# Three tiles side by side, chunk by chunk, at the start of each half of a projection

## The chip, the cores and the metric

The kernel runs on one core of a Trainium2 chip. The metric is the time of one execution on the device in microseconds (us); lower is better. Times of the kernel before are the median of three runs. One further execution was recorded by the hardware profiler, and all rows below come from it.

## The reference

A trunk of two decoder layers is run for one prompt (512 positions) and for 8 samples of 8 positions each (64 rows), 576 columns in all, with a width of 1024. The reference in its bare shape:

```python
h = rmsnorm(x, norm_mix_pre)
m = mixer(h)                         # even layer: attention and S5; odd layer: Mamba-2
x = x + rmsnorm(m, norm_mix_post)
h = rmsnorm(x, norm_mlp_pre)
a = relu(h @ w_up)                   # 1024 -> 4096
x = x + rmsnorm((a * a) @ w_down, norm_mlp_post)
```

Layer 0 is even, layer 1 is odd; each is followed by the MLP of the last three lines. All arithmetic is f32. `rmsnorm` divides every column by the root of its mean square, so nothing that reads `h` of a column can start before the sum of squares over all 1024 features of `x` is there.

## The kernel before

**Products.** Activations lie transposed: features on the partitions in 8 chunks of 128, positions along the free axis, cut into two halves of 288 columns (`HV`). Each f32 product is made of three matmuls in a rounded f32 form, `wh*xh`, `wh*xl` and `wl*xh`, where `h` is the rounded value and `l` the rest (L326, L347, L348). One output tile of 128 features by 288 columns is 3 x 8 chunks = 24 matmuls into one PSUM bank. The pool `mm`, from which `project3_steps` takes its banks, has three banks in this part of the program (`LATE_BANKS`, L1592); a fourth tile can start only when the bank of the first has been read.

**Weights.** For each tile SP's queue loads a 128 x 1024 block (`w`); ACT rounds it to `wh` (L290), VectorE (DVE) subtracts to `wl` (L312). A pair `wh`, `wl` serves both halves.

**Half by half.** `rounds(..., first=n)` makes one round in which `n` tiles are run for half 0 and then the same `n` tiles for half 1. There are three such stretches: the first segment of each MLP's up product (`LEAD` = 8 tiles) and the start of the odd layer's input projection (`lead`, five tiles: 40, 32, 36, 16, 17). Elsewhere a tile's two halves follow one another. A half-by-half stretch stands where the columns of half 1 are not ready yet: while half 0 is multiplied, the post-norm and pre-norm of half 1 run on the other engines. These are, in `add_normed` and what it calls, eight scalings `m = m * normw * nr` on DVE (L381), eight additions to the residual (L395; chunks 1, 4 and 7 on POOL, the others on DVE), eight weightings `h` on ACT and DVE (L403), squares on ACT with sums on POOL and DVE (L203), and two small matmuls `rstd` (L211) that add the squares over the partitions.

**Evacuation.** In `up` DVE reads the bank first (`m` or `a2t` = max(ps, 0) times the column's factor, L1006), ACT squares (L287), ACT and DVE split into two parts (L290, L355), and in half 1 POOL takes differences (L1014). POOL also forms sums and differences of the down weights (`ws`, L1070). After the eighth tile of half 1 `down_pairs` begins. In the odd layer the lead's first tile (40) is the raw time step `dtr` (L1172), from which a chain on DVE leads to `dt_post` (L1247).

**Order.** Every engine works through its own list in order. The lists are fixed when the program is built: a scheduler simulates the program and orders the instructions of each engine, so a change in one place can move instructions on all of them.

Of the kernel before, what the change touches and what calls it, by code (L numbers as in the profile page):

```python
# [21 lines left out]
HV = ((0, HALF), (HALF, T))  # L22
# [195 lines left out]
class _Kernel:  # L218
# [106 lines left out]
                    es.enter_context(self.tc.issue_after(ins))  # L325
            self.nc.tensor.matmul(*args, **kw)  # L326

    def project3(self, *args):
        for _ in self.project3_steps(*args):
            pass  # L330

    def project3_steps(self, src, rounds, kchunk, evac, ready=None, ring=lambda m: None):


        for steps in rounds:
            parts, ready = ready or {}, None
            for m, hf in steps:
                if m not in parts:
                    parts[m] = self.split_block(src(m), ring(m))
                wh, wl = parts[m]  # L340
                lo, hi = HV[hf]
                ps = self.mmps("project3")
                out = ps[:, : hi - lo]
                for c in range(8):
                    xh, xl = kchunk(c, hf)
                    self.product(c, out, wh[:, c, :], xh, start=(c == 0), stop=False)
                    self.nc.tensor.matmul(out, wh[:, c, :], xl, start=False, stop=False)  # L347
                    self.nc.tensor.matmul(out, wl[:, c, :], xh, start=False, stop=(c == 7))  # L348
                self.groups += 1
                evac(m, hf, out)  # L350
                yield

    def split_into(self, hi, lo, t):
        self.copy_a(hi, t)
# [70 lines left out]
    def even(self):  # L425
# [3 lines left out]
        with ExitStack() as es:  # L429
# [5 lines left out]
            for _ in range(N_WARM):  # L435
                nc.tensor.matmul(ps[:, :128], self.ones, self.ones, start=True, stop=True)
            self.wp = ev, NSE
            w = a["w_in_e"]
# [155 lines left out]
    def attn_sample(self, pair, qk, qbd, pnew):  # L594
# [8 lines left out]
        def ring():  # L603
            nb[0] += 1
            ways = RINGS[pair]
            return {"k": (self.eb, "kv", NKV), "w": None, "h": (ev, "wh", NSE), "l": (ev, "wl", NSE)}[ways[nb[0] % len(ways)]]

# [377 lines left out]
    def mlp(self, layer, h, r, mx, done):  # L985

        m = self.halves(self.mring)
        nc = self.nc  # L990
        sums = [_Squares(self, 8, SQ_M[hf]) for hf in range(2)]
        up_w, dn_w = self.a[f"w_up{layer}"], self.a[f"w_dn{layer}"]
        e1 = [mx.tile([128, HALF], F32, tag=f"e1{i}", name=self.nm("e1"), bufs=1) for i in range(4)]
        for seg in range(4):
            last = seg == 3
            act = {k: [mx.tile([128, 4 * HALF], F32R, tag=f"a{k}{p}", name=self.nm(f"a{k}"), bufs=1)
                       .rearrange("p (a b) -> p a b", a=4) for p in "hl"]
                   for k in (("11", "21", "22", "t1") if last else ("11", "21", "22", "t1", "t2", "t3", "t4"))}
            names = {(0, 0): "11", (1, 0): "21", (0, 1): "t1", (1, 1): "22"}
            keep = {}  # L1000

            def up(i, hf, ps):
                kh, j = divmod(i % 8, 4)

                t = m[0][:, i, :] if seg == 0 and hf == 0 else mx.tile([128, HALF], F32, tag="a2t", name=self.nm("a2t"), bufs=NC)
                nc.vector.scalar_tensor_tensor(t, ps, 0.0, r[hf], op0=ALU.max, op1=ALU.mult)  # L1006
                self.act(t, t, ACTF.Square)
                keep[kh, hf, j] = t
                part = lambda k: [p[:, j, :] for p in act[k]]
                if last or (kh, hf) != (0, 1):  # L1010
                    self.split_into(*part(names[kh, hf]), t)
                if not last and hf == 1:

                    sub = lambda o, a, b: nc.gpsimd.tensor_tensor(o, a, b, ALU.subtract)  # L1014
                    if kh == 0:
                        t1 = keep["t1", j] = mx.tile([128, HALF], F32, tag="a2t", name=self.nm("a2t"), bufs=NC)
                        sub(t1, t, keep[0, 0, j])
                        self.split_into(*part("t1"), t1)
                    else:
                        t1, b12, b21 = keep["t1", j], keep[0, 1, j], keep[1, 0, j]  # L1020
                        sub(t1, t, t1)
                        self.split_into(*part("t2"), t1)
                        sub(b12, t, b12)
                        self.split_into(*part("t3"), b12)
                        sub(b21, b21, t1)
                        self.split_into(*part("t4"), b21)

            mts = [8 * seg + i for i in ((0, 4, 1, 5, 2, 6, 3, 7) if not last else range(8))]
            self.share = 0 if seg else SHARE_LEAD
            if seg == 0:  # L1030
                self.spare = [2, 3, 4]
            self.project3(lambda i: up_w[i, 0], self.rounds(mts, first=0 if seg else LEAD), self.chunk(h), up)

            if not last:
                self.down_pairs(lambda i: dn_w[i, seg], act, m, e1, seg == 0, mx)
                continue
            self.spare = [2, 3, 4]

            for i in range(4):
                for o in (m[0][:, 2 * i + 1, :], m[1][:, 2 * i, :], m[1][:, 2 * i + 1, :]):  # L1040
                    nc.gpsimd.tensor_tensor(o, o, e1[i], ALU.add)

            def down(i, hf, ps):
                out = m[hf][:, i, :]
                nc.vector.tensor_tensor(out, out, ps, ALU.add)
                sums[hf].add(out)
                if i == 7:
                    done(hf, m[hf], sums[hf])

            self.project3(lambda i: dn_w[i, seg], self.rounds(range(8), last=TAIL),  # L1050
                          lambda c, hf: [p[:, c % 4, :] for p in act[names[c // 4, hf]]], down)
# [60 lines left out]
    def odd(self, h, spill, done):  # L1112
# [3 lines left out]
        with ExitStack() as es:  # L1116
            ol = es.enter_context(tc.tile_pool(name="ol", bufs=1, reuse_waits="tile"))
            od = es.enter_context(tc.tile_pool(name="od", bufs=1, reuse_waits="tile"))
            self.od = od
            self.wp = es.enter_context(tc.tile_pool(name="ow", bufs=1, side="right", reuse_waits="tile")), NSO  # L1120
            self.share = SHARE_ODD
# [73 lines left out]
            hc = self.chunk(h)  # L1195
            src = lambda m: a["w_dt"][0, 0] if m == 40 else w[m, 0]
# [74 lines left out]
            m = self.halves(self.mring)  # L1271
# [31 lines left out]
            lead = [40, 32, 36, 16, 17]  # L1303
            ready = {m: self.split_block(src(m)) for m in lead[:NSO]}
            ow = self.wp
            with tc.tile_pool(name="ld", bufs=1, reuse_waits="tile") as ld:
                self.wp, self.share = (ld, len(lead) - NSO), SHARE_LEAD
                self.project3(src, self.rounds(lead, first=len(lead)), hc, evac, ready)
            self.oa = es.enter_context(tc.tile_pool(name="oa", bufs=1, reuse_waits="tile"))
            self.wp, self.share = ow, SHARE_ODD  # L1310
            proj([18, 19])
# [297 lines left out]
SQ_G = "pv"  # L1609
NS = 5  # L1610
NSE = 2
NSO = 2
NHB = 4
SHARE_ODD = 3
# [31 lines left out]
LEAD = 8  # L1646
# [40 lines left out]
```

## Time and profile before

| | us |
|---|---|
| Median of 3 runs | 1770.38 |
| Lowest, highest | 1768.38, 1774.1 |
| Profiled execution, its own time | 1776.06 |
| Its span | 1773.9 |
| PE busy (TensorE matmuls) | 1665.1 (94%) |
| DVE busy (VectorE) | 1190.5 (67%) |
| ACT busy (ScalarE) | 770.9 (43%) |
| POOL busy (GpSimd) | 670.4 (38%) |

Shares of busy time are means over stages that differ. A stretch is read from its own rows: on PE a bracket at the end of a row gives the idle time just ahead of it and the instruction that ended it. The span begins at 0; the stretches that the change touches lie at about 386 to 436 us (first MLP), 790 to 850 us (odd layer) and 1355 to 1418 us (second MLP).

### The profile page before, as it was taken

Reading aid. Unit: us, or ns where it says so; the run is one execution under the profiler, and the core shown is the slowest. Engines: PE = TensorE matmul, PEld = TensorE weight load, DVE = VectorE, ACT = ScalarE, POOL = GpSimd, SP = SyncE. Lnnn points to the kernel's source line nnn. Section 1 sums busy time; section 2 is a strip of 40 time slices with the busy share of each in tenths; the row PEclk is TensorE's granted clock in tenths of the full one; section 3 lists DMA queues with packets and bytes.
Section 4 is the critical chain, followed back from the end, with each engine's and each line's share of the span. In section 5 each row is a group of like instructions: output and inputs, shape, how many; then the busy total and the mean of one; then the engine's idle time right before and its main releaser. Section 6 shows DMA issues by size and latency. Waiting matters only on the chain.

```text
span 1773.9 us, 31866 instructions
## 1 busy us (share of the span) xinstructions
PE 1665.1 (94%) x12719; PEld 1532.1 (86%) x12719; DVE 1190.5 (67%) x2045; ACT 770.9 (43%) x1506; POOL 670.4 (38%) x705
## 2 busy tenths in 40 slices
PE   8998999899999999998799899999977999999997
PEld 8875565799999999997789789899857999999996
DVE  8656434467668676358788866977667866767634
ACT  5233433455554444334325536335245555344431
POOL 3533100245445362034365434442344644436102
PEclk9999899899999999999899999999978999999999
DMA  8568554530232313223142141241513033231311
GB/s 276 108 227 308 187 191 163 183 97 13 84 107 72 120 48 120 84 67 111 48 139 82 48 161 60 81 147 53 188 59 126 29 93 98 72 119 48 120 59 54
DMA packets 81652, 197.42 MB, mean 111 GB/s; under 512 B 20352, under 2 KB 32000, under 8 KB 81504
## 3 DMA queue, kind: packets, MB, share of 16 engines
q1 hardware_dynamic: 57568, 174.72, 29.8%
q10 hardware_dynamic: 23936, 20.67, 4.0%
q8 instruction: 100, 1.64, 0.4%
q14 instruction: 48, 0.39, 0.1%
HBM read 176.92 MB, written 18.44 MB: 110 GB/s over the span
## 4 chain that ended last, share of the span: by engine, by line
PE 38%; DVE 7%; ACT 2%; POOL 2%; issue 1%; DMA 1%; DVEq 0%; ACTq 0%; POOLq 0%
PE project L326 7%; PE project L347 7%; PE project L348 7%; PE pair L1100 2%; PE pair L1101 2%; PE pair L1102 2%; PE out_proj L1291 2%; PE out_proj L1289 2%; PE out_proj L1290 2%; PE ssd_group L1499 1%; DVE m L381 1%; DVE wl L312 1%; PE ssd_group L1420 1%; PE ssd_group L1454 1%; DVE cacc L1143 1%
## 5 line engine op out<-in xcount | busy, mean ns | idle before, releaser
L326 PE MATMUL project<-h,wh 128*128 128x288 f32 x1808 | 545.9, 303 | 26.8 <-ACT wh L290 9.7
L347 PE MATMUL project<-h,wh 128*128 128x288 f32 x1808 | 544.8, 302 | 7.0 <-DVE h L403 6.6
L348 PE MATMUL project<-h,wl 128*128 128x288 f32 x1808 | 542.0, 301 | 2.9 <-DVE wl L312 2.9
L326 PEld LDWEIGHTS project<-h,wh 128*128 128x128 f32 x1808 | 346.1, 192 | 38.9 <-ACT wh L290 11.7
L347 PEld LDWEIGHTS project<-h,wh 128*128 128x128 f32 x1808 | 347.1, 192 | 16.0 <-DVE h L403 9.2
L290 ACT ACTIVATE wh<-w 128x1024 fp32r<-128x1024 f32 (+1 forms) x239 | 216.6, 920 | 325.4 <-PE pair L1101 94.6
L348 PEld LDWEIGHTS project<-h,wl 128*128 128x128 f32 x1808 | 346.2, 192 | 10.0 <-issue 4.2
L312 DVE TENSOR_TENSOR wl<-w,wh 128x1024 fp32r<-128x1024 f32 (+1 forms) x148 | 189.3, 1285 | 104.1 <-ACT wh L290 101.6
L203 POOL TENSOR_TENSOR nacc<-nacc,nsq 128x288 f32<-128x288 f32 x88 | 83.1, 945 | 249.2 <-ACT nsq L287 235.6
L1014 POOL TENSOR_TENSOR a2t<-a2t,a2t 128x288 f32<-128x288 f32 x80 | 83.9, 1065 | 172.6 <-ACT a2t L287 167.8
L1101 PE MATMUL pair<-at,wh 128*128 128x288 f32 x384 | 112.8, 296 | 1.1 <-DVE at L355 1.1
L1102 PE MATMUL pair<-at,wl 128*128 128x288 f32 x384 | 111.7, 295 | 0.0
L1100 PE MATMUL pair<-at,wh 128*128 128x288 f32 x384 | 111.3, 295 | 0.0
L355 DVE TENSOR_TENSOR at<-a2t,at 128x288 fp32r<-128x288 f32 x96 | 65.8, 689 | 34.6 <-ACT at L290 34.6
L1067 DVE TENSOR_TENSOR wl<-ws,wh 128x512 fp32r<-128x512 f32 x96 | 83.0, 903 | 4.3 <-ACT wh L290 3.5
L1100 PE MATMUL pair<-a,wh 128*128 128x288 f32 x288 | 85.2, 296 | 0.6 <-DVE a2t L1006 0.6
L1101 PE MATMUL pair<-a,wh 128*128 128x288 f32 x288 | 84.8, 295 | 0.0
L1102 PE MATMUL pair<-a,wl 128*128 128x288 f32 x288 | 84.4, 295 | 0.5 <-DVE wl L1067 0.5
L1289 PE MATMUL out_proj<-x,wh 128*128 128x288 f32 x256 | 77.4, 304 | 3.0 <-DVE m L1296 2.5
L1143 DVE SCALAR_TENSOR_TENSOR cacc<-raw,cw,cacc 128x600 f32<-128x600 f32 x72 | 69.7, 968 | 13.5 <-POOL cacc L1141 12.5
L1291 PE MATMUL out_proj<-x,wl 128*128 128x288 f32 x256 | 76.9, 304 | 0.7 <-POOL wl L312 0.4
L1290 PE MATMUL out_proj<-x,wh 128*128 128x288 f32 x256 | 76.9, 301 | 0.0
(522 smaller groups left out, 3904.4 us busy)
## 6 DMA issues: line engine op xcount, KB each, us to landing
w<-in_w_dn SPq DMA_DIRECT2D x64, 512.0 KB, 3.5
w<-in_w_up SPq DMA_DIRECT2D x64, 512.0 KB, 3.5
w<-in_ck SPq DMA_DIRECT2D x40, 512.0 KB, 5.5
w<-in_cv SPq DMA_DIRECT2D x40, 512.0 KB, 5.8
w<-in_w_in_o SPq DMA_DIRECT2D x40, 512.0 KB, 3.5
w<-in_w_out_o SPq DMA_DIRECT2D x20, 512.0 KB, 3.5
hb<-in_h SPq DMA_DIRECT2D x32, 256.0 KB, 3.7
out_ssm_s<-hn ACTq DMA_DIRECT2D x32, 256.0 KB, 3.6
```

The costliest lines, as they stand in the source:

```text
L290: return self.nc.scalar.activation(out, in_, ACTF.Identity, **kw)
L312: eng.tensor_tensor(f(lo), f(raw), f(hi).bitcast(F32), ALU.subtract)
L326: self.nc.tensor.matmul(*args, **kw)
L347: self.nc.tensor.matmul(out, wh[:, c, :], xl, start=False, stop=False)
L348: self.nc.tensor.matmul(out, wl[:, c, :], xh, start=False, stop=(c == 7))
L1100: nc.tensor.matmul(ps, wh, xh, **(dict(start=True) if p in begin and c == 0 else go_on), stop=False)
L1101: nc.tensor.matmul(ps, wh, xl, **go_on, stop=False)
L1102: nc.tensor.matmul(ps, wl, xh, **go_on, stop=c == 3)
L1143: stt(acc, raw[:, k:k + 600], cw[:, 4 * m + k:4 * m + k + 1], acc, op0=ALU.mult, op1=ALU.add)
L1289: nc.tensor.matmul(out, wh[:, c, :], gh[:, k, :], start=(k == 0), stop=False)
L1290: nc.tensor.matmul(out, wh[:, c, :], gl[:, k, :], start=False, stop=False)
L1291: nc.tensor.matmul(out, wl[:, c, :], gh[:, k, :], start=False, stop=(k == 3))
```

## The change

In the first MLP segment and in the odd lead, the tiles at positions 0, 1, 2 of each half (`wide` holds the positions 0 and 8, or 0 and 5, at which a group starts) are taken as a group of `WIDE` = 3. The group takes three banks at once. For each chunk `c` all three tiles of the group issue their three matmuls before chunk `c + 1` begins; only then are the three tiles handed to `evac`, in order. The number of matmuls, their operands and everything else are the same. In other rounds a group is one tile, as before.

```diff
-    def project3_steps(self, src, rounds, kchunk, evac, ready=None, ring=lambda m: None):
+    def project3_steps(self, src, rounds, kchunk, evac, ready=None, ring=lambda m: None, wide=None):
         for steps in rounds:
             parts, ready = ready or {}, None
-            for m, hf in steps:
-                if m not in parts:
-                    parts[m] = self.split_block(src(m), ring(m))
-                wh, wl = parts[m]
-                lo, hi = HV[hf]
-                ps = self.mmps("project3")
-                out = ps[:, : hi - lo]
+            i = 0
+            while i < len(steps):
+                n = WIDE if wide and i in wide else 1
+                group, outs = steps[i:i + n], []
+                i += n
+                for m, hf in group:
+                    if m not in parts:
+                        parts[m] = self.split_block(src(m), ring(m))
+                    lo, hi = HV[hf]
+                    outs.append(self.mmps("project3")[:, : hi - lo])
                 for c in range(8):
-                    xh, xl = kchunk(c, hf)
-                    self.product(c, out, wh[:, c, :], xh, start=(c == 0), stop=False)
-                    ...
-                self.groups += 1
-                evac(m, hf, out)
-                yield
+                    for (m, hf), out in zip(group, outs):
+                        wh, wl = parts[m]
+                        xh, xl = kchunk(c, hf)
+                        self.product(c, out, wh[:, c, :], xh, start=(c == 0), stop=False)
+                        ...
+                for (m, hf), out in zip(group, outs):
+                    self.groups += 1
+                    evac(m, hf, out)
+                    yield
...
-            self.project3(lambda i: up_w[i, 0], self.rounds(mts, first=0 if seg else LEAD), self.chunk(h), up)
+            self.project3(lambda i: up_w[i, 0], self.rounds(mts, first=0 if seg else LEAD), self.chunk(h), up,
+                          wide=None if seg else (0, 8))
...
-                self.project3(src, self.rounds(lead, first=len(lead)), hc, evac, ready)
+                self.project3(src, self.rounds(lead, first=len(lead)), hc, evac, ready, wide=(0, len(lead)))
...
+WIDE = 3
```

**TensorE, first MLP, start of half 0.** The first tile is `project_674`, the second `project_678`, the third `project_682`. Before, the end of the first tile and the start of the second:

```order
L326 MATMUL project_674_4207<-h_3816,wh_4203 128x288
L347 MATMUL project_674_4207<-h_3817,wh_4203 128x288
L348 MATMUL project_674_4207<-h_3816,wl_4204 128x288
L326 MATMUL project_678_4242<-h_3816,wh_4238 128x288
L347 MATMUL project_678_4242<-h_3817,wh_4238 128x288
L348 MATMUL project_678_4242<-h_3816,wl_4239 128x288
```

The changed kernel from its first matmul of the same half (its line numbers are 7 or 8 higher):

```order
L326 MATMUL project_674_4207<-h_3816,wh_4203 128x288
L354 MATMUL project_674_4207<-h_3817,wh_4203 128x288
L355 MATMUL project_674_4207<-h_3816,wl_4204 128x288
L326 MATMUL project_678_4214<-h_3816,wh_4210 128x288
L354 MATMUL project_678_4214<-h_3817,wh_4210 128x288
L355 MATMUL project_678_4214<-h_3816,wl_4211 128x288
```

Before, 24 rows of one tile follow each other and then 24 of the next. Now two tiles alternate by three rows for four chunks; then stand eleven rows of the third tile, the two `rstd` matmuls of the post-norm of half 1, and the rest of all three in turn, so that all three end in the last nine rows of the 72. The scheduler keeps the two `rstd` matmuls at the same distance from the start of the half.

**DVE, first MLP, the same half.** `m_4181` is the evacuation, `m_3536` and `x_3510` are the post-norm and the residual of half 1, `a_...` the split of a squared tile. Before:

```order
L312 TENSOR_TENSOR wl_4449<-w_4446,wh_4448 128x1024
L1006 SCALAR_TENSOR_TENSOR m_4181<-project_674_4207,nht_3855 128x288
L355 TENSOR_TENSOR a_658_4188<-m_4181,a_657_4187 128x288
L381 SCALAR_TENSOR_TENSOR m_3536<-m_3536,normw,nr_4118 128x288 x8
L1006 SCALAR_TENSOR_TENSOR m_4181<-project_678_4242,nht_3855 128x288
L395 TENSOR_TENSOR x_3510<-x_3510,m_3536 128x288 x5
L1006 SCALAR_TENSOR_TENSOR m_4181<-project_682_4277,nht_3855 128x288
```

And now:

```order
L312 TENSOR_TENSOR wl_4449<-w_4446,wh_4448 128x1024
L389 SCALAR_TENSOR_TENSOR m_3536<-m_3536,normw,nr_4118 128x288 x8
L403 TENSOR_TENSOR x_3510<-x_3510,m_3536 128x288 x4
L1014 SCALAR_TENSOR_TENSOR m_4181<-project_674_4207,nht_3855 128x288
L1014 SCALAR_TENSOR_TENSOR m_4181<-project_678_4214,nht_3855 128x288
L403 TENSOR_TENSOR x_3510<-x_3510,m_3536 128x288
L1014 SCALAR_TENSOR_TENSOR m_4181<-project_682_4221,nht_3855 128x288
```

The evacuation of the first tile moved from ahead of the eight scalings to behind them and behind four additions; the split `a_658` moved out of this piece to a later row.

**DVE, second MLP, end of half 0.** `m_14593` is the evacuation (tiles 2219, 2223, 2227, 2231 are the fifth to the eighth), `m_8711` and `h_14054` are the post-norm and residual of half 1, `x_14515` its weighted chunks. Before:

```order
L381 SCALAR_TENSOR_TENSOR m_8711<-m_8711,normw,nr_14519 128x288 x8
L395 TENSOR_TENSOR h_14054<-h_14054,m_8711 128x288
L355 TENSOR_TENSOR a_2189_14602<-m_14593,a_2188_14601 128x288
L395 TENSOR_TENSOR h_14054<-h_14054,m_8711 128x288 x2
L1006 SCALAR_TENSOR_TENSOR m_14593<-project_2219_14759,nht_14328 128x288
L395 TENSOR_TENSOR h_14054<-h_14054,m_8711 128x288 x2
L403 SCALAR_TENSOR_TENSOR x_14515<-h_14054,normw,x_14514 128x288 x2
L1006 SCALAR_TENSOR_TENSOR m_14593<-project_2223_14794,nht_14328 128x288
L403 SCALAR_TENSOR_TENSOR x_14515<-h_14054,normw,x_14514 128x288 x6
L1006 SCALAR_TENSOR_TENSOR m_14593<-project_2227_14829,nht_14328 128x288
```

And now:

```order
L389 SCALAR_TENSOR_TENSOR m_8711<-m_8711,normw,nr_14519 128x288 x8
L403 TENSOR_TENSOR h_14054<-h_14054,m_8711 128x288
L1014 SCALAR_TENSOR_TENSOR m_14593<-project_2219_14759,nht_14328 128x288
L403 TENSOR_TENSOR h_14054<-h_14054,m_8711 128x288 x4
L1014 SCALAR_TENSOR_TENSOR m_14593<-project_2223_14794,nht_14328 128x288
L411 SCALAR_TENSOR_TENSOR x_14515<-h_14054,normw,x_14514 128x288 x3
L1014 SCALAR_TENSOR_TENSOR m_14593<-project_2227_14829,nht_14328 128x288
L411 SCALAR_TENSOR_TENSOR x_14515<-h_14054,normw,x_14514 128x288 x5
L363 TENSOR_TENSOR a_2187_14600<-m_14593,a_2186_14599 128x288
L1014 SCALAR_TENSOR_TENSOR m_14593<-project_2231_14864,nht_14328 128x288
```

The evacuations of the fifth to seventh tile moved up between the additions and weightings; that of the eighth stands behind all weightings, as before.

## Rows read from the trace of the kernel before

**Rows 1.** The page: busy time by engine; granted TensorE clock in 40 slices.
```profile
PE 1665.1 (94%) x12719; PEld 1532.1 (86%) x12719; DVE 1190.5 (67%) x2045; ACT 770.9 (43%) x1506; POOL 670.4 (38%) x705
...
PEclk9999899899999999999899999999978999999999
```

**Rows 2.** PE timeline, first MLP: start, us, line, tile, count, [idle before <-releaser].
```profile
391.79 1.24 PE L211 MATMUL rstd<-nacc,ones 128*128 128x288 f32 x4 [1.15 <-POOL nacc L203]
...
394.61 0.29 PE L326 MATMUL project<-h,wh 128*128 128x288 f32 x1
...
397.80 0.30 PE L326 MATMUL project<-h,wh 128*128 128x288 f32 x1
...
403.25 0.40 PE L326 MATMUL project<-h,wh 128*128 128x288 f32 x1 [2.09 <-DVE m L1006]
...
415.07 0.75 PE L211 MATMUL rstd<-nacc,ones 128*128 128x288 f32 x2 [0.70 <-POOL nacc L203]
...
419.10 0.30 PE L326 MATMUL project<-h,wh 128*128 128x288 f32 x1
```

**Rows 3.** DVE timeline, first MLP, half 0.
```profile
394.58 0.46 DVE L1006 SCALAR_TENSOR_TENSOR m<-project,nht 128x288 f32<-128x288 f32 x1
396.02 1.25 DVE L355 TENSOR_TENSOR a<-m,a 128x288 fp32r<-128x288 f32 x1 [0.99 <-ACT a L290]
397.19 5.64 DVE L381 SCALAR_TENSOR_TENSOR m<-m,normw,nr 128x288 f32<-128x288 f32 x8
402.75 0.45 DVE L1006 SCALAR_TENSOR_TENSOR m<-project,nht 128x288 f32<-128x288 f32 x1
403.12 2.99 DVE L395 TENSOR_TENSOR x<-x,m 128x288 f32<-128x288 f32 x5
```

**Rows 4.** ACT timeline, first MLP: the factor `nr` for the scalings.
```profile
395.89 0.48 ACT L287 ACTIVATE nr<-rstd,eps 128x288 f32<-128x288 f32 x1
```

**Rows 5.** POOL timeline, first MLP: last of three sums of down weights.
```profile
396.91 1.50 POOL L1070 TENSOR_TENSOR ws<-w,ws 128x512 f32<-128x512 f32 x1
```

**Rows 6.** Stretches: us, then busy PE, PEld, DVE, ACT, POOL, PEclk, DMA share, GB/s.
```profile
403.60:407.00 3.40, 3.40 (x16) 3.40 (x15) 3.40 (x8) 3.02 (x9) 1.32 (x3) 0.50 0.00 0
419.00:436.00 17.00, 17.00 (x129) 17.00 (x129) 9.12 (x17) 7.99 (x18) 6.86 (x8) 1.00 0.06 17
...
822.30:846.20 23.90, 17.59 (x134) 17.36 (x132) 22.63 (x31) 10.38 (x19) 15.18 (x13) 0.95 0.33 111
1398.40:1426.00 27.60, 26.88 (x199) 26.21 (x197) 25.22 (x35) 15.66 (x37) 19.89 (x19) 1.00 0.13 40
```

**Rows 7.** PE timeline, odd lead: first matmul of half 1; `dt_post`.
```profile
814.09 0.66 PE L326 MATMUL project<-h,wh 128*128 128x288 f32 x3 [2.09 <-ACT h L290]
846.16 0.74 PE L1247 MATMUL dt_post<-ident,tq 96*128 96x96 f32 x3 [6.31 <-DVE tq L1241]
```

**Rows 8.** DVE timeline, odd lead: a weight split; half 1's first evacuation.
```profile
802.38 1.21 DVE L312 TENSOR_TENSOR wl<-w,wh 128x1024 fp32r<-128x1024 f32 x1
...
822.30 0.52 DVE L1172 TENSOR_SCALAR dtr<-project,po 96x288 f32<-96x288 f32 x1 [1.85 <-PE project L348]
```

**Rows 9.** PE timeline, second MLP: eighth tile of half 0, half 1.
```profile
1386.97 0.37 PE L326 MATMUL project<-h,wh 128*128 128x288 f32 x1 [2.03 <-DVE m L1006]
...
1393.66 0.40 PE L347 MATMUL project<-x,wh 128*128 128x288 f32 x1 [0.89 <-DVE x L403]
...
1396.68 0.75 PE L211 MATMUL rstd<-nacc,ones 128*128 128x288 f32 x2 [0.47 <-POOL nacc L203]
...
1402.47 0.30 PE L326 MATMUL project<-x,wh 128*128 128x288 f32 x1
```

**Rows 10.** DVE timeline, second MLP.
```profile
1376.04 7.74 DVE L381 SCALAR_TENSOR_TENSOR m<-m,normw,nr 128x288 f32<-128x288 f32 x8
...
1389.18 4.86 DVE L403 SCALAR_TENSOR_TENSOR x<-h,normw,x 128x288 fp32r<-128x288 f32 x6
1393.96 0.45 DVE L1006 SCALAR_TENSOR_TENSOR m<-project,nht 128x288 f32<-128x288 f32 x1
...
1395.06 0.45 DVE L1006 SCALAR_TENSOR_TENSOR m<-project,nht 128x288 f32<-128x288 f32 x1
...
1398.49 0.46 DVE L1006 SCALAR_TENSOR_TENSOR a2t<-project,nht 128x288 f32<-128x288 f32 x1 [1.49 <-ACT nht L287]
```

More of the change, by code (lines that the diff above doesn't have):

```diff
@@ L326, in product, with project3 @@
             self.nc.tensor.matmul(*args, **kw)
-    def project3(self, *args):
-        for _ in self.project3_steps(*args):
+    def project3(self, *args, **kw):
+        for _ in self.project3_steps(*args, **kw):
             pass
-    def project3_steps(self, src, rounds, kchunk, evac, ready=None, ring=lambda m: None):
+    def project3_steps(self, src, rounds, kchunk, evac, ready=None, ring=lambda m: None, wide=None):
         for steps in rounds:
             parts, ready = ready or {}, None
-            for m, hf in steps:
-                if m not in parts:
-                    parts[m] = self.split_block(src(m), ring(m))
-                wh, wl = parts[m]
-                lo, hi = HV[hf]
-                ps = self.mmps("project3")
-                out = ps[:, : hi - lo]
-                for c in range(8):
-                    xh, xl = kchunk(c, hf)
-                    self.product(c, out, wh[:, c, :], xh, start=(c == 0), stop=False)
-                    self.nc.tensor.matmul(out, wh[:, c, :], xl, start=False, stop=False)
-                    self.nc.tensor.matmul(out, wl[:, c, :], xh, start=False, stop=(c == 7))
-                self.groups += 1
-                evac(m, hf, out)
-                yield
+            i = 0
[8 more added lines that the diff above has]
+                    outs.append(self.mmps("project3")[:, : hi - lo])
+                for c in range(8):
+                    for (m, hf), out in zip(group, outs):
+                        wh, wl = parts[m]
+                        xh, xl = kchunk(c, hf)
+                        self.product(c, out, wh[:, c, :], xh, start=(c == 0), stop=False)
+                        self.nc.tensor.matmul(out, wh[:, c, :], xl, start=False, stop=False)
+                        self.nc.tensor.matmul(out, wl[:, c, :], xh, start=False, stop=(c == 7))
+                for (m, hf), out in zip(group, outs):
+                    self.groups += 1
+                    evac(m, hf, out)
+                    yield
     def split_into(self, hi, lo, t):
```

## The prediction

> **What bounds the kernel now.** I read the page first: TensorE is busy for 94% of the span and its granted clock is at or near full in most slices [rows 1]. So the kernel is a row of matmuls with holes, and a change that keeps every matmul can act only on the holes, and on the clock around them. Next I read the TensorE timeline of the three stretches that the change touches, looking for brackets. In the first MLP's half 0 there are three: 1.15 us ahead of the two `rstd` matmuls, 2.09 us ahead of the fifth tile (it waits for DVE to read the bank of the second tile), 0.70 us ahead of the second `rstd` [rows 2]. In the odd layer half 1 begins after 2.09 us on ACT's `h`, and `dt_post` waits 6.31 us for the time-step chain on DVE [rows 7]. In the second MLP the eighth tile waits 2.03 us for a bank, half 1 waits 0.89 us for a chunk and 0.47 us for a sum [rows 9]. Last I read DVE, which ends most of these waits: in the first MLP one evacuation stands between eight scalings and five additions [rows 3].
>
> What the change could gain there: when chunks of half 1 come one at a time, three tiles use up each chunk before the next is wanted. It can take away the 0.89 us and part of what follows. What it must cost: three banks fill together and come free together, at the end of 72 matmuls rather than one after each 24, and a fourth tile has no bank until the first of the group is read.
>
> **The change part by part.** No matmul, load or evacuation is added or removed; a tile of 24 takes 397.80 - 394.61 = 3.19 us [rows 2], 0.133 us for each matmul.
>
> *First MLP, half 0.* The chunks of half 0 are all there, so nothing is waited for that a group could shorten. Before, the fourth tile started at 397.80 with no wait. Now it needs the evacuation of the first tile, and that stands on DVE behind eight scalings and four additions. When does it end? The scalings need `nr`, whose first step began at 395.89, after the square and the split of the first tile [rows 4]; both of these now come later, so `nr` moves ahead and the scalings can follow the `wl` split that ends where the old evacuation began, at 394.6, rather than at 397.19 [rows 3]. From there 5.64 us of scalings, 4 x 2.99/5 = 2.4 us of additions and 0.45 us of evacuation [rows 3] give 394.6 + 8.5 = 403.1. But POOL works on its sums until 396.91 + 1.50 = 398.4 [rows 5], and the DVE split that lay beside them took 1.25 us [rows 3] where others take 0.45; four of the scalings' microseconds now lie beside POOL and only 1.2 did before. With 0.8 us for that I take 403.9. Bounds: all thirteen at 0.45 us gives 394.6 + 5.9 = 400.5; scalings as slow as in the second MLP, 7.74 us [rows 10], give 405.2. I stay near the first reading since its duration is from the same place.
>
> From the fourth tile's start five tiles remain: 5 x 3.19 = 16.0 us. Ahead of the old fifth tile the bank wait of 2.09 us was followed by 3.4 us at a granted clock of 0.50 [rows 6], the lower of the two levels (1.2 of 2.4 GHz): such a stretch costs about half its length, 1.6 us as I count it. The new wait begins near 397.5 and lasts some 6 us, so I keep that 1.6. With 0.4 us for two `rstd` matmuls half 1 begins at 403.9 + 18.0 = 421.9, and the 0.70 us is gone in this count. It began at 419.10 [rows 2]: +2.8, bounds -0.6 (400.5) and +4.1 (405.2). In other words, the wait for a bank moved one tile forward and takes place with one tile fewer done.
>
> The Trainium skill, "Perfetto Trace Analysis", section "Matmuls", says that independent matmul groups should rotate through PSUM banks so that the evacuation of one overlaps the matmuls of the next. The 2.09 us at 403.25 is such a rotation failing even with tiles in turn, and the change takes the rotation away for the first 72 matmuls. By the rule this edit loses; the rows above give the size.
>
> *First MLP, half 1.* DVE is busy 9.12 of the 17 us [rows 6], so three evacuations that come at once have cover; their bunching can push ACT and POOL work behind. +0.3, bounds 0 and +1.
>
> *Odd lead.* Half 0 loses nothing on TensorE beyond what it already waits for. On DVE the order now puts one split `wl`, 1.21 us [rows 8], ahead of the scalings of half 1's post-norm instead of behind them, and another between the additions; some of it lies in idle time, so I take +0.9 on the start of half 1 [rows 7]. In half 1 the first tile `dtr` ends 6 matmuls before the group's end instead of about 13 before: 7 x 0.133 = +0.95 on its evacuation, which waited for TensorE by 1.85 us already [rows 8]. From there to `dt_post` DVE is busy 22.63 of 23.90 us [rows 6], so a delay at its head arrives at the 6.31 us wait nearly whole. +1.8. Bounds: -1.5 if ACT and DVE get their weight splits done early enough that part of the 2.09 us goes; +4.5 if two splits of 1.21 us more fall into the chain.
>
> *Second MLP.* In half 0 the second `rstd` matmul of half 1's post-norm stands nine rows later, 9 x 0.133 = +1.2 us, and the scalings with it. The evacuations of tiles five to seven moved up, so the eighth tile starts about 0.5 us earlier. In half 1 the group needs all three banks: those of tiles seven and eight of half 0, which DVE reads between and behind the weightings (1393.96 and 1395.06 [rows 10]). The 0.89 us on a chunk and the 0.47 us on the sum [rows 9] turn into bank waits: about 1.0 us for the second tile and 0.8 to 2.7 us for the third, since the weightings (4.86 us for six, [rows 10]) start later by the 1.2. The group then ends near 1403.0, where the fourth tile began at 1402.47. The first evacuation of half 1, at 1398.49, cannot come before about 1402.1, and from there DVE is busy 25.22 of 27.60 us [rows 6]: it hardly catches up 3.6 us. Of these TensorE can hide what the three banks hold, about one half. +2.0, bounds -1 and +4.
>
> Sum: 2.8 + 0.3 + 1.8 + 2.0 = +6.9 on the profiled execution's 1776.06, that is 1783.0. That execution lies 5.7 above the median of the runs; on the median the same sum gives 1770.4 + 6.9 = 1777.3.
>
> **The rivals.**
> (a) The other side: DVE runs at its quick pace. If nothing beside it slows DVE, the first tile's evacuation is done at 400.5 (-0.6) and that of the eighth tile in the second MLP before 1394, so that half 1 keeps its gain of 0.89 + 0.47 + 0.5 = 1.9; with the odd lead at its lower bound that is -0.6 - 1.9 - 1.5 = -4.0, or 1766.4. It decides at 401.1: an evacuation before that leaves half 1 of the first MLP no later than now. For it speaks that thirteen short operations need only 5.9 us; against it that scalings took 5.64 and 7.74 us for eight, never 3.6.
> (b) A larger loss: the waits grow, and each new one of 2 us or more brings another stretch at half clock, 3.4 us long and 1.6 us dear as at 403.6 [rows 6], at two more places, +3.2, with the odd chain at +4.5 instead of +1.8: 6.9 + 3.2 + 2.7 = +12.8, or 1783.2. For it speaks 403.25; against it the 2.03 us wait at 1386.97, after which the eighth tile took its normal time.
> (c) The change does little: the lists are written by a scheduler that already mixes rows of tiles where chunks come late, and the long waits (6.31 us, clock windows) stay. Then losses and gains within 2 us, 1770.4. Against it stands the order on DVE, where the evacuation has plainly moved.
>
> **How the numbers follow.** Forecast 0.50, (a) 0.15, (b) 0.20, (c) 0.15. A difference of 0.3%, 5.3 us, is about what can be told from none. The forecast's own range, with its terms spread within their bounds, is +3 to +10: 0.35 of its 0.50 lies over 5.3 and 0.15 within. Rival (b) is slower whole. (a) gives 0.10 to faster, where another stretch gains too, and 0.05 to the same; (c) gives all to the same. Slower 0.55, same 0.35, faster 0.10. The range from 1768 to 1785 holds the forecast, (b), (c) and leaves out most of (a).
>
> **What would show it.** In the profile after: a bank wait of about 6 us ahead of the first MLP's fourth tile in place of 2.09 ahead of the fifth, and half 1 there near 422; no wait on a chunk in the second MLP's half 1 but one or two on `m`; its first evacuation about 3.6 us after the place it had; `dt_post` about 2 us later against the start of the odd stretch. The prediction is wrong if the bank wait is short (the evacuation ends by 401), or if the gain in the second MLP stays whole.

## The result, and the profile after

The changed kernel takes 1782.24 us (median of 13 runs), the kernel before 1771.50 us in 13 runs beside it: ratio 1.0056, 95% interval 1.0035 to 1.0076, that is +9.9 us (+6 to +13). Slower, as forecast; 1777.3 was predicted, with a range of 1768 to 1785. The profiled execution has a span of 1780.4 us, 6.5 above the one before.

The first rows of the page after show the same busy time and nearly the same clock:

```profile
PE 1668.5 (94%) x12719; PEld 1534.2 (86%) x12719; DVE 1189.2 (67%) x2045; ACT 768.7 (43%) x1506; POOL 666.3 (37%) x705
...
PEclk9899989899999999999899999999968999999998
```

TensorE works 3.4 us more [rows 1], a part of which is matmuls at the lower clock; the rest of the loss is idle time. The PE timeline of the first MLP's half 0 shows where (start, us, engine, line, tile, count, idle time ahead):

```profile
381.66 0.30 PE L326 MATMUL project<-h,wh 128*128 128x288 f32 x1
...
382.88 0.40 PE L326 MATMUL project<-h,wh 128*128 128x288 f32 x1 [0.66 <-ACT m L290]
...
387.27 1.24 PE L211 MATMUL rstd<-nacc,ones 128*128 128x288 f32 x4
...
400.50 0.61 PE L326 MATMUL project<-h,wh 128*128 128x288 f32 x1 [7.10 <-DVE m L1014]
...
413.13 0.65 PE L211 MATMUL rstd<-nacc,ones 128*128 128x288 f32 x2
...
419.48 0.30 PE L326 MATMUL project<-h,wh 128*128 128x288 f32 x1
```

The 72 matmuls of the group have one hole: three matmuls in, the second tile waits 0.66 us until ACT has read a bank of the product before (`m`, L290), since the group wants three banks at once. Then TensorE stands 7.10 us until DVE has read the first tile. The brackets of 1.15, 2.09 and 0.70 us [rows 2] are gone. From the first matmul of half 0 to that of half 1 it is 419.48 - 381.66 = 37.82 us; before, the half took 33.29. DVE in the same stretch, and POOL's last sum of weights ahead of its additions:

```profile
389.55 7.13 DVE L389 SCALAR_TENSOR_TENSOR m<-m,normw,nr 128x288 f32<-128x288 f32 x8
396.60 3.35 DVE L403 TENSOR_TENSOR x<-x,m 128x288 f32<-128x288 f32 x4
399.99 0.82 DVE L1014 SCALAR_TENSOR_TENSOR m<-project,nht 128x288 f32<-128x288 f32 x2
```
```profile
393.93 1.48 POOL L1079 TENSOR_TENSOR ws<-w,ws 128x512 f32<-128x512 f32 x1
```

The evacuation at 399.99 has its tile complete since 393; it stands behind eight scalings that took 7.13 us, where they took 5.64 [rows 3], and four additions. The longer time goes with POOL: beside the eight scalings it is busy for 5.79 us now and for 3.24 us before (after, then before; us, then busy PE, PEld, DVE, ACT, POOL, ...):

```profile
389.55:396.68 7.13, 3.85 (x30) 3.62 (x28) 7.13 (x10) 0.28 (x1) 5.79 (x5) 0.93 0.23 76
```
```profile
397.19:402.83 5.64, 3.97 (x30) 3.74 (x29) 5.64 (x10) 1.41 (x3) 3.24 (x3) 1.00 0.02 6
```

In both kernels a scaling that began while POOL was idle took 0.51 us, one that began while POOL worked 1.04 to 1.56 us. Then the fourth tile runs at about half clock (granted 0.53):

```profile
400.50:406.20 5.70, 5.70 (x24) 5.70 (x25) 5.70 (x9) 4.06 (x12) 3.94 (x5) 0.53 0.00 0
```

In half 1 no row of PE has a bracket until the down pairs, but two of these wait 0.93 and 0.90 us for an evacuation; before, the first did not wait and the second 0.29. Counted from the start of the half, the changed kernel is 1.05 us late at the first of the two and 2.33 us at the second. After, then before:

```profile
447.73 0.37 PE L1109 MATMUL pair<-at,wh 128*128 128x288 f32 x1 [0.93 <-DVE a2t L1014]
...
451.84 0.37 PE L1109 MATMUL pair<-a,wh 128*128 128x288 f32 x1 [0.90 <-DVE a2t L1014]
```
```profile
449.14 0.37 PE L1100 MATMUL pair<-a,wh 128*128 128x288 f32 x1 [0.29 <-DVE a2t L1006]
```

The second MLP shows the same exchange. After:

```profile
1391.21 0.37 PE L326 MATMUL project<-h,wh 128*128 128x288 f32 x1 [0.96 <-DVE m L1014]
...
1395.59 0.40 PE L326 MATMUL project<-x,wh 128*128 128x288 f32 x1 [0.56 <-DVE m L1014]
...
1399.64 0.40 PE L326 MATMUL project<-x,wh 128*128 128x288 f32 x1 [0.85 <-DVE m L1014]
...
1425.26 0.38 PE L1109 MATMUL pair<-at,wh 128*128 128x288 f32 x1 [0.96 <-DVE a2t L1014]
...
1429.39 0.37 PE L1109 MATMUL pair<-a,wh 128*128 128x288 f32 x1 [0.90 <-DVE a2t L1014]
```

The waits on a chunk and on the sum [rows 9] have gone, and bank waits of 0.56 and 0.85 us stand there; the pairs wait 0.96 and 0.90 us where before only the second had a bracket:

```profile
1422.90 0.37 PE L1100 MATMUL pair<-a,wh 128*128 128x288 f32 x1 [0.28 <-DVE a2t L1006]
```

**How the stretches are compared.** From the start to the first MLP TensorE's instructions are the same in all kernels below that leave the banks alone, yet the first matmul of that MLP came anywhere from 375.9 to 388.8 us in their profiled executions. So spans are not compared; lengths of stretches are, each the difference of two starts on the PE timeline, of the same two places in the order. A: first MLP, first matmul of half 0 to first of half 1. B: from there 368 matmuls on, into the pairs (the products with the down weights). C: odd lead, first matmul of half 1 to `dt_post`. D: second MLP, 576 matmuls from its first one (the `rstd` matmuls not counted), both halves and the first pairs.

| kernel | A | B | C | D | ratio to before (95%) |
|---|---|---|---|---|---|
| before | 33.29 | 51.30 | 32.08 | 96.47 | 1 |
| changed | 37.82 | 53.62 | 33.98 | 97.67 | 1.0035 to 1.0076 |
| e1, first MLP half 0 only | 38.16 | 51.29 | 32.06 | 96.43 | 1.0011 to 1.0043 |
| e2, first MLP half 1 only | 33.56 | 53.63 | 32.00 | 97.01 | 0.9969 to 1.0014 |
| e3, odd lead only | 32.87 | 51.29 | 34.03 | 97.29 | 0.9962 to 1.0013 |
| e4, second MLP only | 33.53 | 51.28 | 32.06 | 98.68 | 0.9988 to 1.0040 |
| e5, groups of two | 35.03 | 51.26 | 32.45 | 97.01 | 0.9989 to 1.0040 |
| e6, four banks | 34.93 | 53.87 | - | - | one run |
| e7, staggered ends | 35.14 | 51.98 | 33.67 | 97.27 | 0.9983 to 1.0035 |
| e8, ACT reads the group | 34.49 | 53.66 | 34.03 | 96.91 | one run |
| e9, before, ACT reads | 32.99 | 51.28 | 32.09 | 97.09 | 0.9960 to 0.9996 |
| e10, time-step tile alone | 33.11 | 51.30 | 32.07 | 97.02 | one run |
| e11, before, ACT reads, first MLP | 35.31 | 51.30 | 32.07 | 97.20 | 0.9976 to 1.0021 |

Where a stretch is not touched, A scatters from 32.9 to 33.6, B by 0.02, C by 0.1 and D from 96.4 to 97.3. A term smaller than that is not read from it. (e3 counts as untouched in D, though the scheduler gave its second MLP another order too.)

D falls into two parts that differ in this. Up to the fourth tile of half 1 it took 52.1 to 53.9 us where the second MLP is not wide, and 51.1 to 52.9 us where it is (changed, e4, e8). From there on it took 45.8 us in these three, and 43.3 us in before, e1, e2, e5, e9, e10 and e11. e7 has 44.0, and e3 45.2, of which a part is 3.4 us at the lower clock.

### The profile page after: what moved, and what is told of

It is laid out like the page before. It is cut to its first block, busy times and chain, and to the rows that moved or that the text cites. A ratio compares the mean times of both kernels' runs of the same rounds, so it can differ in the third digit from the quotient of the medians.

```text
span 1780.4 us, 31857 instructions
## 1 busy us (share of the span) xinstructions
PE 1668.5 (94%) x12719; PEld 1534.2 (86%) x12719; DVE 1189.2 (67%) x2045; ACT 768.7 (43%) x1506; POOL 666.3 (37%) x705
## 4 chain that ended last, share of the span: by engine, by line
PE 67%; DVE 17%; ACT 5%; DMA 5%; issue 3%; POOL 2%; ACTq 0%; SPq 0%; DVEq 0%; POOLq 0%
PE project L326 13%; PE project L354 12%; PE project L355 12%; PE pair L1109 5%; PE pair L1110 5%; PE pair L1111 5%; DVE wl L312 2%; DVE cacc L1152 2%; DVE m L389 2%; PE out_proj L1299 2%; PE out_proj L1298 2%; PE out_proj L1300 2%; PE ssd_group L1508 1%; DVE at L363 1%; PE s L931 1%
## 5 line engine op out<-in xcount | busy, mean ns | idle before, releaser
L290 ACT ACTIVATE wh<-w 128x1024 fp32r<-128x1024 f32 (+1 forms) x239 | 216.7, 920 | 332.7 <-PE pair L1110 95.4
L1298 PE MATMUL out_proj<-x,wh 128*128 128x288 f32 x256 | 77.3, 304 | 3.2 <-DVE m L1305 2.7
L1014 DVE SCALAR_TENSOR_TENSOR a2t<-project,nht 128x288 f32<-128x288 f32 x112 | 50.2, 451 | 42.6 <-PE project L355 42.2
L326 PE MATMUL project<-x,wh 128*128 128x288 f32 x256 | 76.0, 297 | 1.4 <-DVE m L1014 1.4
```

The costliest lines, as they stand in the source:

```text
L290: return self.nc.scalar.activation(out, in_, ACTF.Identity, **kw)
L1298: nc.tensor.matmul(out, wh[:, c, :], gh[:, k, :], start=(k == 0), stop=False)
```

## The experiments

**e1 to e4: one stretch at a time.** Only the argument `wide` differs from the changed kernel. Edits (in this order):

```diff
-                          wide=None if seg else (0, 8))
+                          wide=(0,) if seg == 0 and layer == 0 else None)     # e1, odd lead wide=None
+                          wide=(8,) if seg == 0 and layer == 0 else None)     # e2, odd lead wide=None
+                          wide=None)                                          # e3
+                          wide=(0, 8) if seg == 0 and layer == 1 else None)   # e4, odd lead wide=None
```

Expected of e1:

> Only the first MLP's half 0 goes three tiles wide. Theory: the loss there is the bank wait ahead of the fourth tile (the evacuation stands behind the scalings), whatever the other stretches do: about 7 us of wait, first matmul of half 0 to first matmul of half 1 37.8 us against 33.3 (+4.5), and half 1 up to the down pairs as before (within 0.5 of it). Rival: half 1 starts on a late DVE, so part of the +2.3 that half 1 showed comes along with half 0 alone. Whole kernel +4.5 us, or +6.8 by the rival.

Measured: A +4.87, B -0.01, and a bank wait as in the changed kernel. The theory holds and the rival falls: half 1's loss does not come along with half 0.

```profile
395.30 0.61 PE L326 MATMUL project<-h,wh 128*128 128x288 f32 x1 [6.66 <-DVE m L1014]
```

Expected of e2:

> Only the first MLP's half 1 goes three tiles wide. Theory: half 0 stays at 33.3 us; in half 1 the first evacuation comes some 5.9 us later (at the 66th matmul rather than the 24th), three come at once, DVE loses that time before a stretch in which it has none to spare, and the down pairs begin 2 to 2.5 us later. Rival: bunching is harmless because DVE is only half busy in the 17 us after the start of half 1, and the +2.3 came from half 0: then within 0.3 us of before.

Measured: A +0.27, B +2.33, as in the changed kernel (+2.32). Three evacuations come at once after DVE had waited 6.84 us for TensorE; where the tiles go in turn (e1), one comes alone 24 matmuls in. The rows of e2 and of e1:

```profile
422.73 1.26 DVE L1014 SCALAR_TENSOR_TENSOR a2t<-project,nht 128x288 f32<-128x288 f32 x3 [6.84 <-PE project L355]
```
```profile
417.45 0.46 DVE L1014 SCALAR_TENSOR_TENSOR a2t<-project,nht 128x288 f32<-128x288 f32 x1 [1.29 <-PE project L355]
```

Half 1 begins at 413.78 in e2 and 414.05 in e1, so the first evacuation comes 8.95 and 3.40 us after it. The rival falls. The whole time of e2 does not show the 2.3 us; they lie within its interval.

Expected of e3:

> Only the odd lead goes three tiles wide. Theory: the loss stands up to dt_post (about +3.6 us: +1.7 up to the start of half 1, +1.9 on the time-step chain), and the order behind it adds or gives back within 1 us. Rival: the +3.6 is carried in from other stretches' scheduling; then within 1 us of before up to dt_post.

Measured: C +1.95 as in the changed kernel (+1.90). The +1.7 ahead of half 1 came to +0.7 here, while e1, which has nothing wide in that stretch, shows +1.6 there: that part is scatter, a miss of the expectation.

Expected of e4:

> Only the second MLP goes three tiles wide. Theory: about +0.7 us in all: half 0 about 1.5 us shorter (chunk and bank waits shorter), half 1 up to the pairs about 2.2 us longer (evacuations bunched). Rival: the 1.5 us of half 0 were luck of the clock; then +2.2 in all.

Measured: D +2.21, as the rival had it. But the second MLP untouched scatters by 0.9 (e1 to e11), the changed kernel has +1.2 and e8, wide there too, +0.4. What is settled is the second part of D: +2.5 us from the fourth tile of half 1 on, in e4 as in the changed kernel and e8. Whether the part ahead of it gains anything is lost in its scatter.

**e6: a fourth bank.**

```diff
-LATE_BANKS = dict(mm=3, ax=2, tr=1, acc=1, dac=1)
+LATE_BANKS = dict(mm=4, ax=1, tr=1, acc=1, dac=1)
```

Expected:

> The changed kernel with four mm banks in place of three (the ax pool, which the rstd sums use, has one instead of two). Theory: in the first MLP the fourth tile takes the fourth bank and starts right behind the group; the long wait moves to the fifth tile and still ends when DVE has read the first tile, so with one tile more done half 0 takes about 3.2 us less than in the changed kernel: 34.6 us (before 33.3, changed 37.8). Half 1 keeps its +2.3 since its evacuations still come at once. Rival: the bank is not what is short but DVE's time; then a fourth bank moves nothing and half 0 stays at 37 to 38 us.

Measured: A 34.93, B +2.57. The fourth tile starts without a wait and the fifth waits:

```profile
413.20 0.61 PE L326 MATMUL project<-h,wh 128*128 128x288 f32 x1 [3.45 <-DVE m L1014]
```

The number of banks decides which tile waits. The kernel as a whole took 1901 us, and between `dt_post` and the second MLP, where one bank of `ax` is left, it needs some 100 us more than before. What costs there is not shown; only A and B are read from this kernel.

**e7: the same start, staggered ends.**

```diff
-                for c in range(8):
-                    for (m, hf), out in zip(group, outs):
+                runs = [(c, g) for c in range(4) for g in range(n)] + [(c, g) for g in range(n) for c in range(4, 8)]
+                for c, g in runs:
+                    (m, hf), out = group[g], outs[g]
                     ...
```

Expected:

> The changed kernel, but the group goes chunk by chunk for chunks 0 to 3 only; then each tile finishes its chunks 4 to 7 by itself, so that the three tiles end 12 matmuls apart. On DVE the first evacuation of the first MLP now stands behind the eight scalings but ahead of the additions. Theory: the bank wait ahead of the fourth tile shrinks by the additions, from 7.1 to about 3.8 us, half 0 34 to 35 us (changed 37.8); in half 1 the first evacuation comes 48 matmuls in rather than 66, and the loss of 2.3 us up to the pairs falls to about 1. Rival: what costs is that three banks are taken at once, whatever the order of their ends: no change from the changed kernel (half 0 37 to 38, half 1 +2.3).

Measured: A 35.14, a wait of 4.34 us, B +0.67. Of the 4.5 us in half 0 the stagger gives back 2.7, of the 2.3 in half 1 1.65. The rival falls: with three banks still taken at once, an earlier end of the first tile gives most of the loss back.

```profile
405.89 0.61 PE L326 MATMUL project<-h,wh 128*128 128x288 f32 x1 [4.34 <-DVE m L1015]
```

**e8: another engine reads the banks.**

```diff
-                nc.vector.scalar_tensor_tensor(t, ps, 0.0, r[hf], op0=ALU.max, op1=ALU.mult)
+                if layer == 0 and seg == 0 and hf == 0 and i in (0, 4, 1):
+                    self.act(t, ps, ACTF.Relu)
+                    nc.vector.tensor_tensor(t, t, r[hf], ALU.mult)
+                else:
+                    nc.vector.scalar_tensor_tensor(t, ps, 0.0, r[hf], op0=ALU.max, op1=ALU.mult)
```

Expected:

> The changed kernel, but the banks of the first MLP's first group (half 0) are read by ACT (relu into SBUF); DVE multiplies by the column's factor afterwards. ACT's first read stands behind one weighting of half 1. Theory: the wait ahead of the fourth tile ends with ACT's read, about 3 us sooner than the 400.5 of the changed kernel's clock, so about 4 us of wait and half 0 near 34.8 us (changed 37.8). Rival: DVE is the bound of half 1's pre-norm anyway, and the wait reappears ahead of a later tile or of half 1: half 0 37 us or more.

Measured: A 34.49, and the wait ends with ACT:

```profile
394.91 0.40 PE L326 MATMUL project<-h,wh 128*128 128x288 f32 x1 [3.79 <-ACT m L287]
```

So what stands ahead of the evacuation in DVE's order makes the wait longer: with ACT as the reader it is 3.79 us instead of 7.10, and it does not come back elsewhere in A. B stays at +2.36, since half 1 is unchanged.

**e10: the time-step tile out of the group.** Both MLPs tile after tile (`wide=None`), and in the odd lead:

```diff
-                self.project3(src, self.rounds(lead, first=len(lead)), hc, evac, ready, wide=(0, len(lead)))
+                self.project3(src, self.rounds(lead, first=len(lead)), hc, evac, ready, wide=(1, 1 + len(lead)))
```

Expected:

> Only the odd lead is wide, and its group begins at the second tile: the time-step tile stands alone again and ends 58 matmuls after the first of half 1, as before (65 where it is in the group). Theory: its later end is what holds dt_post back, since the DVE chain from it has no slack: first matmul of half 1 to dt_post back to 32.1 us, from 34.0 with the tile in the group. Rival: the 7 matmuls explain 0.9 us only and the rest comes from the other work on DVE and POOL: about 33 us. Second rival: the bank shortage in half 1 costs it, whichever tiles are in the group: 34 us.

Measured: C 32.07, the value of before to 0.01 us, and `dtr` is read 8.2 us after the start of half 1, as before. But this does not show the theory for the whole of the +1.9: the 7 matmuls explain 0.93 us only, and the granted clock at the start of half 1 differs as well. Changed kernel, before, e10 (us, busy PE and count, ..., clock third from the end):

```profile
818.50:822.50 4.00, 4.00 (x18) 3.94 (x19) 3.84 (x9) 2.09 (x5) 0.00 (x0) 0.57 0.01 4
```
```profile
814.09:818.00 3.91, 3.91 (x29) 3.85 (x30) 3.75 (x9) 2.00 (x5) 0.00 (x0) 1.00 0.02 4
```
```profile
812.57:816.00 3.43, 3.43 (x25) 3.37 (x26) 3.35 (x8) 1.52 (x4) 0.00 (x0) 1.00 0.02 5
```

18 matmuls in 4.00 us against 29 in 3.91: 11 x 0.133 = 1.5 us. With 0.9 that makes the 2.4 us by which the evacuation of `dtr` comes later after the start of half 1 (829.12 - 818.50 = 10.6 against 8.2); DVE's chain gives 0.5 back.

```profile
829.12 0.51 DVE L1181 TENSOR_SCALAR dtr<-project,po 96x288 f32<-96x288 f32 x1 [4.27 <-PE project L355]
```

Two other kernels hold the two causes apart. In e7 `dtr` ends one matmul later than before, at the lower clock: C +1.6. In e5 (groups of two) it ends three matmuls later, at full clock: C +0.4. The same stretch in e7, then in e5:

```profile
820.90:824.90 4.00, 4.00 (x20) 3.94 (x21) 3.84 (x9) 2.09 (x5) 0.00 (x0) 0.67 0.02 4
```
```profile
810.53:814.53 4.00, 4.00 (x29) 3.94 (x30) 3.84 (x9) 2.09 (x5) 0.00 (x0) 1.00 0.01 4
```

So the larger part of the +1.9 is the clock. All thirteen kernels have the same wait of 2.09 or 2.10 us just ahead. Behind it the clock fell in the five whose time-step tile stands in a group of three (changed, e3, e6, e7, e8: 0.57 to 0.67 over 4 us) and in none of the other eight (1.00). Each is one execution; whether the group brings the lower clock, and by what, is not shown.

**e5: groups of two.**

```diff
-WIDE = 3
+WIDE = 2
```

Expected:

> The changed kernel with groups of two tiles instead of three: the third bank stays free for the next tile, and the pair ends 48 matmuls in. Theory: in the first MLP the third tile starts without a wait; the fourth waits for the first evacuation, which now stands behind the scalings but ahead of the additions, about 4 us: half 0 34 to 35.5 us (before 33.3, three tiles 37.8). In half 1 the first evacuation comes 48 matmuls in rather than 66, so 0.7 us are lost up to the down pairs rather than 2.3. Whole kernel +2 to +6 us. Rival: any group at all costs the same, since the scheduler moves the evacuations behind the scalings in either: half 0 near 37.8, +10 us.

Measured: A 35.03 and a wait of 4.51 us ahead of the fourth tile, near the theory; B +0.0, where 0.7 was expected; ratio 1.0014 (0.9989 to 1.0040), about +2.5 us, inside the +2 to +6, though the interval also includes no change. In C, +0.4. The rival falls: A is not near 37.8.

```profile
396.32 0.61 PE L326 MATMUL project<-h,wh 128*128 128x288 f32 x1 [4.51 <-DVE m L1014]
```

**e9 and e11: the kernel before, with ACT reading some banks.** The edit of e8 in the kernel before, with another condition:

```diff
+                if seg == 0 and hf == 0 and i in ((4, 1), (2, 6, 3))[layer]:     # e9
+                if layer == 0 and seg == 0 and hf == 0 and i in (4, 1, 5):       # e11
```

Expected of e9:

> The kernel before (tile after tile), with ACT in place of DVE reading the banks of the second and third tile of the first MLP's half 0 and of the fifth to seventh tile of the second MLP's. Theory: the waits of 2.09 us (first MLP) and 2.03 us (second MLP) for a bank go, and with the first the 1.6 us at half clock behind it: half 0 of the first MLP 29.7 us against 33.3, the second MLP about 2 us less, the whole some 5 us (0.3%) faster. Rival: the chunks and the sum of half 1 come later because ACT is late, and the waits return there: within 1 us of before.

Measured: ratio 0.9978 (0.9960 to 0.9996), -3.9 us (-7 to -0.7), a little faster than before and, by the two ratios, faster than the changed kernel. The profile does not show the gain where it was expected: A is 32.99, only 0.3 less, and A scatters by more. The 2.09 us and the half clock behind it are gone, but the sum of half 1's post-norm waits 1.85 us (before 1.15 [rows 2]), 3.4 us at a granted clock of 0.55 follow, and a wait of 0.91 us is new:

```profile
385.39 1.71 PE L211 MATMUL rstd<-nacc,ones 128*128 128x288 f32 x4 [1.85 <-POOL nacc L203]
...
403.63 0.40 PE L326 MATMUL project<-h,wh 128*128 128x288 f32 x1 [0.91 <-DVE m L1010]
```
```profile
386.40:389.80 3.40, 3.40 (x16) 3.24 (x15) 2.04 (x3) 1.73 (x4) 1.94 (x2) 0.55 0.40 106
```

Expected of e11:

> The kernel before, tile after tile, with ACT reading the banks of the second to fourth tile of the first MLP's half 0 only. Theory: the 2.09 us wait and the half clock behind it go there, and the 0.91 us wait that showed ahead of the seventh tile with two tiles read by ACT goes as well; the second MLP stays as before. Half 0 30 to 32 us against 33.3, whole kernel 2 to 4 us faster. Rival: the wait moves to the sums of half 1 (rstd): half 0 within 0.5 us of before and no gain.

Measured: ratio 0.9998 (0.9976 to 1.0021), A 35.31, no gain. The rival has the place right and the size too small (it allowed 0.5 us in half 0, and 2.0 came): the wait returns ahead of the second `rstd`, at 2.84 us, because POOL's last sum waits for a square on ACT that stands behind the square of an evacuated tile, and this one waits 2.64 us for DVE's multiplication. On PE, ACT and POOL:

```profile
415.02 0.75 PE L211 MATMUL rstd<-nacc,ones 128*128 128x288 f32 x2 [2.84 <-POOL nacc L203]
```
```profile
412.56 0.81 ACT L287 ACTIVATE m<-m 128x288 f32<-128x288 f32 x2 [2.64 <-DVE m L1008]
```
```profile
414.18 0.79 POOL L203 TENSOR_TENSOR nacc<-nacc,nsq 128x288 f32<-128x288 f32 x1 [2.77 <-ACT nsq L287]
```

Where e9's 3.9 us come from stays open.

## Why the prediction was right

The time lies inside the range, and the largest term came from the wait that was forecast. But two of the four terms were too small, by 1.7 and 2.0 us, and a third is right in sum by luck.

*First MLP, half 0: +2.8 forecast, +4.5 measured.* The mechanism is the one forecast: a bank wait of about 6 us ahead of the fourth tile in place of 2.09 ahead of the fifth (measured 7.10), shown by three edits that shorten it in different ways (e6, e7, e8). Rival (a), which needed the evacuation within 15.3 us of the start of the half, fell: tile four could start at 18.8 (400.50 - 381.66), past the forecast 18.1 and inside the upper bound of 19.4 (403.9 and 405.2 on a clock on which the half began at 385.8). The scalings began earlier than forecast (389.55 - 381.66 = 7.9 us into the half, against 8.8), but took 7.13 us where 5.64 + 0.8 were allowed, and the four additions 3.35 where 2.4 were. The prediction read that only 1.2 us of the scalings lay beside POOL before; it was 3.24 of the 5.64, since POOL's additions run there too, and 5.79 of the 7.13 now. The Trainium skill, "GPSIMD Engine Reference", section "1. Specifications", says that GpSimd shares its SBUF interfaces with VectorE and that VectorE's instructions with two SBUF inputs contend with it; a scaling here reads two tiles, and the trace agrees: 0.51 us for a scaling that began with POOL idle, 1.04 to 1.56 us beside it. The rest of the miss is clock: the fourth tile ran whole at 0.53, 5.70 us instead of 3.19, so 2.5 us where 1.6 were allowed.

That 1.6 us, taken from the stretch at half clock in the kernel before, did not lengthen its half 0. In e2, e3, e4 and e10 no lower clock follows that wait (1.22 to 2.04 us there), and A is 32.87 to 33.56, not 1.6 us less than 33.29: 0.7 us ahead of another tile and 1.1 us instead of 0.70 ahead of the second `rstd` stand in its place. As far as these rows show, half 0 before was held by the sums of half 1, with some slack for TensorE; that fits e9, which took away the wait and the half clock and gained next to nothing in A. In the changed kernel the second `rstd` has no wait, so nothing there takes up the slow tile. e2 behind its wait of 2.04 us:

```profile
397.93:401.33 3.40, 3.40 (x25) 3.32 (x25) 3.40 (x7) 3.02 (x8) 1.32 (x3) 1.00 0.00 0
```

The rule on rotating banks that the prediction weighed (the Trainium skill, "Perfetto Trace Analysis", section "Matmuls") came out as it says: with tiles in turn the bank wait was 2.09 us, with the rotation taken away 7.10.

*First MLP, half 1: +0.3 forecast, +2.3 measured.* This is the term that was mis-sized, and the step behind it was wrong: that DVE is busy 9.12 of the 17 us, "so three evacuations that come at once have cover". The idle half of DVE lies ahead of the group's end, where it has nothing to read; behind it DVE is full, and of the 5.6 us by which the first evacuation comes later after the start of the half (8.95 in e2, 3.40 in e1) 2.3 are seen at the pairs. The trace of before had the row that says so, from 436 us on (us; busy PE, PEld, DVE, ...):

```profile
436.00:455.00 19.00, 17.94 (x128) 16.87 (x126) 17.63 (x23) 10.02 (x25) 14.91 (x13) 1.00 0.20 70
```

DVE is busy 17.63 of those 19 us. The forecast looked 17 us ahead and stopped short of it. e2 shows the term by itself, and e7 (+0.7) and e5 (+0.0) take most or all of it away by an earlier first end. For the second MLP the same prediction had used the right argument (a late first evacuation, then a full DVE) and not carried it over.

*Odd lead: +1.8 forecast, +1.9 measured in C,* right in sum by luck. C begins with half 1, so of the forecast only the +0.95 belongs to it. The 7 matmuls are there, but 0.5 us of their 0.93 does not reach `dt_post`, and 1.5 us at the lower clock, which the forecast did not have, makes up the rest (e10, e7, e5). The +0.9 on the start of half 1 cannot be told from scatter (e1 has +1.6 there with nothing changed).

*Second MLP: +2.0 forecast, +1.2 measured,* inside the bounds. The exchange of waits is as forecast, in both places: chunk and sum out, banks in. Its size is the sum of two parts: from the first matmul of the MLP to the fourth tile of half 1 it is 51.9 us against 53.2, a gain that is no larger than the scatter there, and behind it 2.5 us are lost, as in e4 and e8. The forecast had 2.0 for that loss; the first evacuation of half 1 comes 3.2 us later (3.6 forecast), and with an earlier first end the loss there is smaller, as in B (e7 +0.7, e5 +0.0).

*The sum.* A and B alone make +6.9 of the +9.9 us; with C 8.8, with D 10.0. The agreement of 10.0 with 9.9 is closer than D's scatter of 0.9 and the interval of +6 to +13 can carry. The forecast of 6.9 is low by the 2.0 of half 1 and the 1.7 of half 0, and high by 0.8 in D. Rival (b), half clock at two more places, came in part: one longer stretch in half 0 and one in the odd lead. Rival (c) is refuted by A and B.

The times of e1 to e4 taken alone add up to +0.2%, less than the changed kernel's +0.56%; each has an interval of 0.16 to 0.26% to either side, so they can't say whether the parts add. In A, B and C a part alone shows what the whole shows, to 0.35 us.

## What to carry to other kernels

A group of tiles that share each input chunk frees its banks at the end of the group only. Before grouping, look where the first evacuation will stand in the reading engine's order and what it delays: idle time ahead of the group's end is no cover, only time behind it counts. If tiles are to share chunks, let them share the early ones and end one after another: e7 gave back about two thirds of the loss in A and B. Where chunks come late a group could pay; no kernel here shows a gain from it that is clear of the scatter.

## What was not expected

Behind identical waits the granted clock differed: after some 2.09 us of waiting for ACT's `h` the odd lead's half 1 ran at 1.00 in eight kernels and at 0.57 to 0.67 in five, and these five are the ones with the time-step tile in a group of three. In the first MLP's half 0 a wait of 2.09 us was followed by half clock before, and one of 2.04 us in e2 was not. And the first MLP, with the same instructions ahead of it, began at 375.9 to 388.8 us from one profiled execution to another; that is more than the effect under study, and a comparison of two spans alone would have given +6.5 where the runs give +9.9.
